# A hybrid encoder block on one core: conditioning sums spread over a sweep, decayed queries in another buffer group, block sums formed midway, and the last pair of tiles in its own order

## The chip, the cores and the metric

The kernel runs on one core of one Trainium2 chip. The metric is the device time of one execution in microseconds (us). Three runs of the kernel before took 2403.71 to 2405.92 us, with a median of 2404.65 us.

## What is computed

One encoder layer over 16 prompt tiles and 2 sample tiles of 128 rows each, with d = 1024, four retention heads of 128, and an MLP of width 4096:

```python
mod = silu(c) @ ada_w + ada_b                 # six vectors of 1024 per sequence
h = modulate(rmsnorm(x, norm_mix), sh1, sc1)
u, q, k, v, g = split(h @ w_in)
f = real(fft2(u over sequence and group)) @ w_fnet     # per group
r = retention(rotary(q), rotary(k), v, forward) + retention(..., backward, strict)
r = r * rsqrt(mean(r * r)) * silu(g)
x = x + gt1 * (concat(f, r) @ w_out)
h = modulate(rmsnorm(x, norm_mlp), sh2, sc2)
x = x + gt2 * (square(relu(h @ w_mlp_in)) @ w_mlp_out)
y = rmsnorm(x, norm_final)
```

## The kernel before, in words

Matrix products run as three passes of rounded halves (hi times hi, hi times lo, lo times hi), so each operand is split by a cast on ACT and a subtraction on DVE (line 81). Small products of 128x128 run in plain float32, which the trace counts as two matmuls each. A timeline of the framework sets the order of the instructions on each engine; each engine then takes its queue in order. Loads and stores are issued by SP, whose queue is in order too.

The stages that matter here, with their stretch of the trace:

- Sweep 1 (50 to 220 us) projects u. **Sweep 2** (220 to 450 us, the loop over `order`, tiles 17, 16, 15 down to 0) projects v and k with `w_v` and `w_k`, turns k by its rotary angles (`rotary`, lines 228 to 230: three DVE operations `rt`, `kv`, `kv`), stores `kv` to memory (line 711), runs jobs of the Fourier part, and adds up the backward state (`state_b`). In between stand 32 pieces of the conditioning product (`ada_piece`): each loads 512 KB of `ada_w` into a buffer `ada` and runs two DVE operations of 128x1024 on it (`adacc`, lines 354 and 356). After eight pieces `ada_end` multiplies the sums by ones on PE and copies the result on ACT (`adas`, line 373).
- **Sweep 3** (450 to 755 us, tiles 0 to 17) loads `kv`, projects q and g, and calls `retention` for the tile before and `ret_norm` for the one before that. A tile's queries `q` (and the backward state beside them), its decayed queries `qx` (lines 758 and 760) and its gate `sg` (`silu`, line 859) are tiles of 4 KB per partition in the pool group with the tag `"F"`, of which `w_g` and the decay table `xi` hold all but three. Tag `"S"` is the larger group, used by `h`, `hhi`, `hlo`, `kv`, `ada` and others.
- The output projection follows (755 to 975 us), then **MLP1** (980 to 1671 us): three groups `c` of three pairs of row tiles, and for each of them eight column groups `q`, each giving two blocks of hidden units (`hid`). Products use a seven-product block scheme, so that MLP2 needs seven combinations of the hidden blocks: four are stored and three (`S2` to `S4`) are sums. For the last quarter of the hidden units (`r = 3`) the sums are made in MLP1 (`hs`, `hid`) and all seven are stored to `hidd`; for the others MLP2 makes them from `hr` with four DVE operations for each pair.
- **MLP2** (1671 to 2403 us): four quarters `r` of the hidden units, and nine pairs of row tiles in each. `load_mo` prepares the weights of a quarter from `w_mlp_out` (buffers `t`, `o1`, `o2` in `raw` and `rawb`, results `woB`, `woT`). With `r = 3` each pair is finished: multiplied by the gate, added to `x1`, normalized and stored. For the last pair `finish_block` and `finish_rows` do this block by block.

Of the kernel before, what the change touches and what calls it, by code (L numbers as in the profile page):

```python
# [15 lines left out]
P = 128  # L16
# [15 lines left out]
def encoder(ctx: ExitStack, tc: tile.TileContext, a):  # L32
# [656 lines left out]
    for n, t in enumerate(order):  # L689
# [8 lines left out]
        if n >= 1 and jobs:  # L698
            for f in jobs.pop(0):
                f()  # L700
        if n >= 1:
            ada_piece(*ada_jobs.pop(0))
        for _ in range(0 if n < 11 else 1 if n == 11 else 2 if n < 16 else 3):
            ada_piece(*ada_jobs.pop(0), "F")
        kv = t4("kv", "S")
# [6 lines left out]
        if t not in (0, 16):  # L712
            vz = t2("vz")
            pool.tensor_tensor(out=heads(vz), in0=heads(kv[:, 512:1024]),
                               in1=zc[:, 4:8].unsqueeze(2).to_broadcast([P, H, P]), op=ALU.mult)
            pend = (t, kv, vz)
        if n == 12:
            w_q = load_w_in(512, "V")
# [29 lines left out]
    def retention(t, kv, s_b, q, sg, s_f):  # L748
# [6 lines left out]
        act.copy(qk[:, 0:512], tq)  # L755
        qx = t4("qx", "F")
        if not first:
# [77 lines left out]
    for n, t in enumerate(order2):  # L835
# [25 lines left out]
        if 5 <= n < 13:  # L861
            load_w_out(n - 5)
        if n == NT - 2:
            fetch_d(0)
# [113 lines left out]

    NB = [4] * (NG - 1) + [7]
    hidd = [[dram([NPC, GJ, P, NB[r] * P], "hidd") for r in range(NG)] for _ in range(NC)]  # L980

# [39 lines left out]
    for c in range(NC):  # L1021
        if c:
            left = left_ops()
            for pr in range(NPC):
# [5 lines left out]
                form_left(left, pr, *hab, lambda s: wt("s", s, [P, 512], 4))  # L1030
        for q in range(8):
            w = load_mi(q)
            hid = [wt("hid", "hid", [P, NPC, 4, P], 3) for _ in range(2)]
            at, cp_ = [{}, {}], [{}, {}]
            for i, (ln, rn, bn) in enumerate(STEPS):
                for f in range(2):
# [19 lines left out]
                    elif i == 6:  # L1056
# [4 lines left out]
                        dst = hidd[c][j // GJ][:, j % GJ].rearrange("a p n -> p a n")  # L1061
                        if j // GJ == NG - 1:
                            x = wt("hs", "hs", [P, NPC, 3, P], 2)
                            s2, s3, s4 = (x[:, :, m] for m in range(3))
                            sub(s3, hf[:, :, 0], hf[:, :, 3])
                            add(hf[:, :, 3], hf[:, :, 3], hf[:, :, 2])
                        sp.dma_start(out=dst[:, :, 0:4 * P], in_=hf.rearrange("p a b s -> p a (b s)"))
                        if j // GJ == NG - 1:
                            sub(s2, hf[:, :, 3], hf[:, :, 0])
                            sub(s4, hf[:, :, 1], s2)  # L1070
                            sp.dma_start(out=dst[:, :, 4 * P:7 * P], in_=x.rearrange("p a b s -> p a (b s)"))
# [65 lines left out]

    def finish_block(b, y, x1, ss):
        dve.tensor_tensor(out=y, in0=y, in1=gate[:, halves(b)], op=ALU.mult)
        dve.tensor_tensor(out=y, in0=y, in1=x1[:, halves(b)], op=ALU.add)  # L1140
        act.activation(x1[:, halves(b)], y, AF.Square, accum_out=ss[:, b % 2:b % 2 + 1])  # L1141

    def finish_rows(t, y, ss):
        dve.tensor_tensor(out=ss[:, 2:3], in0=ss[:, 0:1], in1=ss[:, 1:2], op=ALU.add)
        r = rstd_from(ss[:, 2:3], 1, 1.0 / D)
        for b in range(2):
            yb = y[:, 512 * b:512 * b + 512]
            dve.scalar_tensor_tensor(out=yb, in0=yb, scalar=r[:, 0:1], in1=nf[:, halves(b)],
                                     op0=ALU.mult, op1=ALU.mult)
            sp.dma_start(out=xrows("y", t)[:, halves(b)], in_=yb)  # L1150

    for r in range(NG):
        w = load_mo(r)
        if r == NG - 1:
            gate = load_gate(1, 0, lambda s: v1(s, "rawb"))
            nf = v1("nf", "rawb")
            sp.dma_start(out=nf, in_=a["norm_final"].rearrange("(o c) -> o c", o=1).to_broadcast([P, D]))
        for pr in range(NT // 2):
            if r == NG - 1 and pr == NP // 2:
                gate = load_gate(1, 1, lambda s: v1(s, "rawb"))  # L1160
            c, pc = divmod(pr, NPC)
            hv = v1("hr", f"hr{pr % 2}").rearrange("p (j b s) -> p j b s", j=GJ, b=7)
            sp.dma_start(out=hv[:, :, 0:NB[r], :].rearrange("p j b s -> p j (b s)"),
                         in_=hidd[c][r][pc].rearrange("j p n -> p j n"))
            src = {n: hv[:, :, i] for i, n in enumerate(("A11", "A12", "A22", "S1", "S2", "S3", "S4"))}
            if NB[r] == 4:
                sub(src["S3"], src["A11"], src["S1"])
# [8 lines left out]
            if r == NG - 1:  # L1176
                x1 = [v1("x1", "raw") for _ in range(2)]
                for i in range(2):
                    sp.dma_start(out=x1[i], in_=x1d[2 * pr + i])
            at = {}  # L1180
            ss = [tsm([P, 4], "ss") for _ in range(2)] if end else None
            for i, (ln, rn, bn) in enumerate(STEPS):
# [12 lines left out]
                else:  # L1195
                    dve.tensor_tensor(out=acc[:, b_], in0=o, in1=acc[:, b_], op=ALU.add)  # L1196
                if end:
                    if i not in (0, 2, 3):
                        finish_block(b_, acc[:, b_], x1[b_ // 2], ss[b_ // 2])
                    if i > 4:  # L1200
                        finish_rows(2 * pr + b_ // 2, rows[b_ // 2], ss[b_ // 2])
                elif r == NG - 1 and i > 4:
                    finish_tile(2 * pr + b_ // 2, rows[b_ // 2], x1[b_ // 2])
# [77 lines left out]
```

## Time and profile before

| what | us |
|---|---|
| median of three runs | 2404.65 |
| the profiled execution, its own time | 2405.53 |
| its span on the engines | 2403.5 |
| PE busy (97% of the span) | 2326.6 |
| DVE busy (64%) | 1539.2 |
| ACT busy (42%) | 1004.5 |
| POOL busy (5%) | 115.8 |

A row of the timeline gives the start, the busy time, the engine, the line, the operation with what it writes and reads, and how many instructions follow one another; in brackets stands how long the engine sat idle before and what ended that. "PE proj L84" is a matmul that writes the projection bank; "SPq" is a transfer issued by SP. Matmuls are pipelined: a row of n matmuls lasts n steps and the rest of the last one.

### The profile page before, as it was taken

To read this page: it belongs to the slowest core of one execution; us is meant where nothing else is said; L and a number is where in the kernel's file an instruction comes from. 1 tells how busy PE (TensorE), PEld (TensorE's weight loads), DVE (VectorE), ACT (ScalarE), POOL (GpSimd) and SP (SyncE) were. 2 spreads that over 40 slices of the span, in tenths; PEclk is the share of its full clock that TensorE was granted. 3 is DMA by queue.
4 is the path that set the end of the run, shared out by engine and by line. 5 is a ranking of instruction groups with operands and counts; after the bars stand their busy time and mean duration, and the time that the engine had idled before them with its cause. 6 is when DMAs were issued, how large, how long until landed. Compare 5 with 4: busy or idle time off the path is not lost.

```text
span 2403.5 us, 30791 instructions
## 1 busy us (share of the span) xinstructions
PE 2326.6 (97%) x11905; PEld 2033.9 (85%) x11905; DVE 1539.2 (64%) x2254; ACT 1004.5 (42%) x1686; POOL 115.8 (5%) x191
## 2 busy tenths in 40 slices
PE   7999999999999999999999999999899999999998
PEld 4788887788887888999999999998787788787786
DVE  3676768535444754655785577557756867857788
ACT  4842222223333533555665566556334323224332
POOL 0101100011111000000000000000000000000000
PEclk9999999999999999999999999999999999999999
DMA  8647568433333455543453346433534545546774
GB/s 286 215 144 252 188 217 289 171 99 121 119 103 127 140 171 188 167 131 123 154 184 123 127 156 194 136 120 130 191 105 159 200 158 197 188 158 227 276 255 165
DMA packets 183866, 411.69 MB, mean 171 GB/s; under 512 B 12101, under 2 KB 80485, under 8 KB 176809
## 3 DMA queue, kind: packets, MB, share of 16 engines
q1 hardware_dynamic: 182136, 405.68, 49.2%
q0 software_dynamic: 1584, 4.06, 0.6%
q8 instruction: 93, 1.52, 0.3%
q14 instruction: 53, 0.43, 0.1%
HBM read 274.15 MB, written 135.54 MB: 170 GB/s over the span
## 4 chain that ended last, share of the span: by engine, by line
PE 77%; issue 9%; DVE 6%; DMA 5%; ACT 2%; POOL 1%; SPq 0%; POOLq 0%; DVEq 0%; ACTq 0%
PE mX L963 30%; PE proj L84 18%; PE mZ L963 15%; PE mY L963 7%; PE o L84 2%; DMA ada<-ada_w 1%; PE dft L84 1%; PE tr L745 1%; DMA hr<-hidd 1%; DVE woT L81 1%; PE kvf L84 1%; DVE adacc L356 1%; DVE woB L81 1%; PE sc L84 1%; DVE acc L1196 1%
## 5 line engine op out<-in xcount | busy, mean ns | idle before, releaser
L963 PE MATMUL mX<-woT,ho 128*128 128x512 f32 x1296 | 311.5, 390 | 3.7 <-ACT x L1141 1.5
L80 ACT CAST ho<-hr 128x512 fp32r<-128x512 f32 x252 | 153.1, 621 | 343.3 <-PE mX L963 208.7
L963 PEld LDWEIGHTS mX<-woT,ho 128*128 128x128 f32 x1296 | 242.8, 188 | 56.3 <-issue 1.9
L963 PE MATMUL mX<-opS,wT 128*128 128x384 f32 x1152 | 208.0, 334 | 0.0
L84 PE MATMUL proj<-whi,hhi 128*128 128x512 f32 x720 | 190.1, 402 | 18.3 <-ACT hhi L80 9.4
L963 PEld LDWEIGHTS mX<-opS,wT 128*128 128x128 f32 x1152 | 200.4, 188 | 0.0
L81 DVE TENSOR_TENSOR ho<-hr,ho 128x512 fp32r<-128x512 f32 x252 | 170.4, 687 | 39.7 <-ACT ho L80 39.5
L84 PE MATMUL proj<-wlo,hhi 128*128 128x512 f32 x720 | 185.2, 396 | 0.0
L84 PE MATMUL proj<-whi,hlo 128*128 128x512 f32 x720 | 184.4, 393 | 0.0
L84 PEld LDWEIGHTS proj<-whi,hhi 128*128 128x128 f32 x720 | 132.4, 190 | 47.4 <-ACT hhi L80 10.7
L84 PEld LDWEIGHTS proj<-wlo,hhi 128*128 128x128 f32 x720 | 136.1, 191 | 30.7 <-issue 2.5
L84 PEld LDWEIGHTS proj<-whi,hlo 128*128 128x128 f32 x720 | 133.1, 188 | 30.7 <-issue 4.2
L81 DVE TENSOR_TENSOR wB<-mr,wB 128x1024 fp32r<-128x1024 f32 x72 | 88.0, 1222 | 81.1 <-ACT wB L80 81.0
L1196 DVE TENSOR_TENSOR acc<-mX,acc 128x512 f32<-128x512 f32 x117 | 80.0, 687 | 68.5 <-PE mX L963 55.5
L963 PE MATMUL mY<-woB,ho 128*128 128x512 f32 x432 | 112.2, 396 | 10.0 <-ACT woB L80 6.8
L963 PE MATMUL mX<-woB,ho 128*128 128x512 f32 x432 | 110.8, 396 | 5.6 <-ACT ho L80 5.5
L963 PE MATMUL mZ<-woT,ho 128*128 128x512 f32 x432 | 108.9, 392 | 6.3 <-ACT woT L80 5.5
L105 POOL TENSOR_SCALAR rv<-ss 128x1 f32<-128x1 f32 (+1 forms) x72 | 17.9, 248 | 1885.8 <-ACT x L139 1391.9
L80 ACT CAST wB<-mr 128x1024 fp32r<-128x1024 f32 x72 | 75.4, 1047 | 76.0 <-PE mY L963 41.0
L963 PEld LDWEIGHTS mY<-woB,ho 128*128 128x128 f32 x432 | 81.7, 190 | 30.1 <-ACT woB L80 8.3
L963 PE MATMUL mY<-opA,wB 128*128 128x384 f32 x576 | 104.6, 334 | 2.3 <-DVE x L153 2.3
L963 PE MATMUL mX<-opA,wB 128*128 128x384 f32 x576 | 105.5, 334 | 0.0
(251 smaller groups left out, 4368.9 us busy)
## 6 DMA issues: line engine op xcount, KB each, us to landing
mr<-w_mlp_in SPq DMA_DIRECT2D x96, 512.0 KB
hidd<-hid SPq DMA_DIRECT2D x48, 768.0 KB
hr<-hidd SPq DMA_DIRECT2D x27, 1024.0 KB
accd<-acc SPq DMA_DIRECT2D x27, 1024.0 KB
acc<-accd SPq DMA_DIRECT2D x27, 1024.0 KB
ada<-ada_w SPq DMA_DIRECT2D x48, 512.0 KB
h<-hd SPq DMA_DIRECT2D x36, 512.0 KB
x<-x_prompt SPq DMA_DIRECT2D x32, 512.0 KB
```

The source lines that it names most:

```text
L80: act.copy(hi, src)
L81: dve.tensor_tensor(out=lo, in0=src, in1=hi.bitcast(F32), op=ALU.subtract)
L84: pe.matmul(out, l, r, start=first, stop=last)
L105: pool.tensor_scalar(out=v[:, :n], in0=ss[:, :n], scalar1=scale, scalar2=EPS, op0=ALU.mult, op1=ALU.add)
L356: dve.scalar_tensor_tensor(out=acc_[s_], in0=w, scalar=c2[:, k, s_:s_ + 1], in1=acc_[s_], op0=ALU.mult, op1=ALU.add)
L745: pe.transpose(o[:, hs], src[:, hs], ident)
L963: pe.matmul(out, l, r, start=first and fresh, stop=last, skip_group_check=not fresh)
L1196: dve.tensor_tensor(out=acc[:, b_], in0=o, in1=acc[:, b_], op=ALU.add)
```

## The change

1. In sweep 2 the conditioning pieces move from ahead of the projections to behind the rotary and the store of k. One piece stands in each tile from the second on, and a second one in each tile from n = 5 on, in place of one, two or three extra ones from n = 11 on. Two of the 32 pieces now fall into sweep 3.
2. `qx` is allocated in the larger group `"S"` instead of `"F"`.
3. In MLP1 the eight column groups run in the order `QS`, which puts the last quarter's two groups (6 and 7) fourth and fifth. The sums are also made there for the first quarter of the first three pairs (`c = 0`, `r = 0`).
4. The last pair of MLP2 gets a function of its own, `last_pair`: the second gate is loaded ahead (`gate_s`, in `raw`), the products of bank X run as two halves of 256 columns, gate and `x1` are applied before the last product instead of after it, and one half of each row is scaled on ACT.

```diff
@@ sweep 2
-        if n >= 1:
-            ada_piece(*ada_jobs.pop(0))
-        for _ in range(0 if n < 11 else 1 if n == 11 else 2 if n < 16 else 3):
-            ada_piece(*ada_jobs.pop(0), "F")
         kv = t4("kv", "S")
         pv = proj(hl, w_v)
...
             pend = (t, kv, vz)
+        if n >= 1:
+            ada_piece(*ada_jobs.pop(0))
+        if n >= 5:
+            ada_piece(*ada_jobs.pop(0), "S" if n < 11 else "F")
@@ retention
-        qx = t4("qx", "F")
+        qx = t4("qx", "S")
@@ sweep 3
+        if n and ada_jobs:
+            ada_piece(*ada_jobs.pop(0))
@@ MLP1
-    NB = [4] * (NG - 1) + [7]
-    hidd = [[dram([NPC, GJ, P, NB[r] * P], "hidd") for r in range(NG)] for _ in range(NC)]
+    NB = [[7 if r == NG - 1 or c + r == 0 else 4 for r in range(NG)] for c in range(NC)]
+    hidd = [[dram([NPC, GJ, P, NB[c][r] * P], "hidd") for r in range(NG)] for c in range(NC)]
+    QS = (2, 0, 1, 6, 7, 3, 4, 5)
-        for q in range(8):
+        for q in QS:
-                        if j // GJ == NG - 1:
+                        if NB[c][j // GJ] == 7:
@@ MLP2
+    def last_pair(src, acc, x1, rows, w):
...
+        def gate_add(b):
+            y = acc[:, b]
+            dve.tensor_tensor(out=y, in0=y, in1=gate[:, halves(b)], op=ALU.mult)
+            add(y, y, x1[b // 2][:, halves(b)])
+        def square(b, k, c=full):
+            act.activation(junk[:, c], acc[:, b][:, c], AF.Square, scale=1.0 / 32,
+                           accum_out=col(k))
...
+        def rows_out(k, rest, early, late):
+            pool.tensor_tensor(out=col(k), in0=col(k), in1=col(rest), op=ALU.add)
+            pool.tensor_tensor(out=col(k), in0=col(k), in1=mhalf[:, 0:1], op=ALU.pow)
+            r = col(k)
+            y = x1[early // 2][:, halves(early)]
+            act.activation(y, y, AF.Copy, scale=r)
+            dve.scalar_tensor_tensor(out=acc[:, late], in0=acc[:, late], scalar=r, in1=nf[:, halves(late)],
                                      op0=ALU.mult, op1=ALU.mult)
+            store(act, early, y)
+            store(sp, late, acc[:, late])
...
+                at[bn] = [(bank("X"), ha), (bank("X"), hb)] if bn == "X" else [(bank(bn), full)]
...
+                if i < 6:
+                    dve.tensor_tensor(out=y, in0=oo, in1=y, op=ALU.add)
+                else:
+                    t = v1("tg", "raw")[:, 0:256]
+                    dve.tensor_tensor(out=t, in0=oo, in1=gate[:, halves(b_)][:, c], op=ALU.mult)
+                    add(y, y, t)
+                    square(b_, 4 + n, c)
...
-            gate = load_gate(1, 0, lambda s: v1(s, "rawb"))
+            gate, gate_s = (load_gate(1, i, lambda s: v1(s, ("rawb", "raw")[i])) for i in range(2))
...
-                gate = load_gate(1, 1, lambda s: v1(s, "rawb"))
+                gate = gate_s
```

Three places show how the order of the instructions moves.

The first is DVE at the end of sweep 2, around the last two tiles; `kv_3796` before and `kv_3763` now are the same rotated keys (of tile 0). Before:

```order
L239 SCALAR_TENSOR_TENSOR sbn_3664<-sbn_3554,kvb_3659 128x128 x4
L356 SCALAR_TENSOR_TENSOR adacc_3675<-ada_3771,c_101,adacc_3675 128x1024
L356 SCALAR_TENSOR_TENSOR adacc_3673<-ada_3775,c_101,adacc_3673 128x1024
L356 SCALAR_TENSOR_TENSOR adacc_3675<-ada_3775,c_101,adacc_3675 128x1024
L239 SCALAR_TENSOR_TENSOR sbn_3756<-sbn_3664,kvb_3751 128x128 x4
L228 TENSOR_TENSOR rt_3850<-proj_3823,rope_3848 128x512
L229 TENSOR_TENSOR kv_3796<-proj_3823,rope_3848 128x512
L229 TENSOR_TENSOR q_3901<-qr_3902,rope_3904 128x512
L230 TENSOR_TENSOR kv_3796<-kv_3796,rt_3850 128x512
```

Now:

```order
L356 SCALAR_TENSOR_TENSOR adacc_3657<-ada_3823,c_101,adacc_3657 128x1024
L356 SCALAR_TENSOR_TENSOR adacc_3659<-ada_3823,c_101,adacc_3659 128x1024
L228 TENSOR_TENSOR rt_3817<-proj_3790,rope_3815 128x512
L229 TENSOR_TENSOR kv_3763<-proj_3790,rope_3815 128x512
L356 SCALAR_TENSOR_TENSOR adacc_3657<-ada_3827,c_101,adacc_3657 128x1024
L239 SCALAR_TENSOR_TENSOR sbn_3674<-sbn_3586,kvb_3669 128x128 x4
L356 SCALAR_TENSOR_TENSOR adacc_3659<-ada_3827,c_101,adacc_3659 128x1024
L230 TENSOR_TENSOR kv_3763<-kv_3763,rt_3817 128x512
L81 TENSOR_TENSOR hlo_3840<-h_3835,hhi_3839 128x1024
L239 SCALAR_TENSOR_TENSOR sbn_3756<-sbn_3674,kvb_3751 128x128 x4
```

The rotated keys of tile 0 now stand ahead of the last backward state and of the first query's rotation, with two sums between their operations; no conditioning sum stands behind them in sweep 2.

The second is one tile of sweep 3, on DVE and then on PE; `qx_5232` and `o_5241` are the decayed queries and the output of the same tile, `sg_5037` is the gate of the tile before it, `q_5292` the query of the tile after it. DVE before:

```order
L229 TENSOR_TENSOR q_5147<-qr_5148,rope_5150 128x512
L230 TENSOR_TENSOR q_5147<-q_5147,rt_5152 128x512
L228 TENSOR_TENSOR rt_5297<-qr_5293,rope_5295 128x512
L808 SCALAR_TENSOR_TENSOR sg_5037<-sg_5037,rr_5206 128x128 x4
L758 TENSOR_TENSOR qx_5232<-tr_5226,xi_3858 128x512
L760 TENSOR_TENSOR qx_5232<-tr_5226,xi_3858 128x512
L239 SCALAR_TENSOR_TENSOR sfn_5261<-sfn_5116,kvf_5256 128x128 x4
L81 TENSOR_TENSOR hlo_5340<-h_5192,hhi_5339 128x1024
L766 TENSOR_TENSOR qkT_5219<-sc_5235,dec_3856 128x512
```

DVE now:

```order
L808 SCALAR_TENSOR_TENSOR sg_5037<-sg_5037,rr_5206 128x128 x4
L229 TENSOR_TENSOR q_5292<-qr_5293,rope_5295 128x512
L230 TENSOR_TENSOR q_5292<-q_5292,rt_5297 128x512
L228 TENSOR_TENSOR rt_5442<-qr_5438,rope_5440 128x512
L758 TENSOR_TENSOR qx_5232<-tr_5226,xi_3833 128x512
L760 TENSOR_TENSOR qx_5232<-tr_5226,xi_3833 128x512
L239 SCALAR_TENSOR_TENSOR sfn_5261<-sfn_5116,kvf_5256 128x128 x4
L766 TENSOR_TENSOR qkT_5219<-sc_5235,dec_3831 128x512
L81 TENSOR_TENSOR hlo_5340<-h_5192,hhi_5339 128x1024
```

The three rotary operations moved from ahead of the gate's four to between these and the two of `qx`, and they are now those of the tile after. PE in the same tile, where each row of a projection is two matmuls; before:

```order
L84 MATMUL proj_5557<-wlo_3310,hhi_5339 128x512 x2
L84 MATMUL proj_5557<-whi_3291,hlo_5340 128x512 x2
L84 MATMUL proj_5557<-whi_3309,hlo_5340 128x512 x2
L84 MATMUL o_5241<-kv_5045,qkT_5219 128x128
L84 MATMUL o_5241<-sfn_5116,qx_5232 128x128
L84 MATMUL o_5241<-q_5147,qx_5232 128x128
L84 MATMUL proj_5592<-whi_3521,hhi_5339 128x512 x2
```

Now:

```order
L84 MATMUL proj_5557<-wlo_3352,hhi_5339 128x512 x2
L84 MATMUL o_5241<-kv_5045,qkT_5219 128x128
L84 MATMUL o_5241<-sfn_5116,qx_5232 128x128
L84 MATMUL o_5241<-q_5147,qx_5232 128x128
L84 MATMUL proj_5557<-whi_3333,hlo_5340 128x512 x2
L84 MATMUL proj_5557<-whi_3351,hlo_5340 128x512 x2
L84 MATMUL proj_5592<-whi_3553,hhi_5339 128x512 x2
```

The eight matmuls of the q projection with `hlo` moved from ahead of the output's products to behind them, so they now stand between the output and the gate's projection (`proj_5592`).

The third is DVE at the border of MLP1 and MLP2, where the weights of the first quarter and the first pair's hidden blocks are prepared. Before:

```order
L1052 TENSOR_TENSOR hid_14125<-mX_14141,c_14240 128x3x128
L81 TENSOR_TENSOR woB_14420<-o_14465,woB_14420 128x512
L236 TENSOR_TENSOR hr_14533<-hr_14533 128x4x128
L81 TENSOR_TENSOR ho_14540<-hr_14533,ho_14540 128x512
L1054 TENSOR_TENSOR hid_14124<-mZ_14212,c_14196 128x3x128
L233 TENSOR_TENSOR hr_14533<-hr_14533 128x4x128
...
L236 TENSOR_TENSOR hs_14310<-hid_14124 128x3x128
```

Now:

```order
L1058 TENSOR_TENSOR hid_14160<-mZ_14248,c_14232 128x3x128
L1058 TENSOR_TENSOR hid_14161<-mZ_14263,c_14246 128x3x128
L81 TENSOR_TENSOR ho_14560<-hr_14557,ho_14560 128x512
L236 TENSOR_TENSOR t_14511<-o_14512 128x512
L81 TENSOR_TENSOR ho_14577<-hr_14557,ho_14577 128x512
L81 TENSOR_TENSOR ho_14594<-hr_14557,ho_14594 128x512
```

The four operations on `hr` of the first pair and the eight on `hs` and `hid` of the last column groups no longer stand here.

## Rows read from the trace of the kernel before

**Rows 1.** Windows view, 400 to 450 us: length, then busy time of each engine.

```profile
400.00:450.00 50.00, 48.38 (x233) 34.99 (x232) 44.79 (x62) 7.07 (x10) 3.73 (x2) 1.00 0.60 206
```

**Rows 2.** Timeline, 394 to 459 us, the end of sweep 2.

```profile
398.51 0.70 PE L84 MATMUL proj<-whi,hhi 128*128 128x512 f32 x2 [3.34 <-DVE kv L229]
...
446.74 0.59 ACT L373 COPY adas<-ada 128x512 f32<-128x512 f32 x1 [15.87 <-PE ada L84]
...
448.46 0.68 DVE L230 TENSOR_TENSOR kv<-kv,rt 128x512 f32<-128x512 f32 x1
...
449.61 2.11 PE L84 MATMUL proj<-whi,hhi 128*128 128x512 f32 x8 [1.62 <-ACT hhi L80]
...
456.04 0.66 PE L745 MATMUL tr<-ident,kv 128*128 128x128 f32 x4 [1.58 <-DMA kv<-kvd]
```

**Rows 3.** Tile view of `adacc` and of `vz`: durations in ns, least, median, most.

```profile
L356 DVE SCALAR_TENSOR_TENSOR adacc<-ada,c,adacc x56: 1269/1275/2065, 186.3 to 439.4; 128x1024 f32<-128x1024 f32 x56
...
L714 POOL TENSOR_TENSOR vz<-kv,zc x14: 1029/1132/1900, 226.3 to 421.3; 128x512 f32<-128x512 f32 x14
```

**Rows 4.** Waits of PE, 500 to 700 and 700 to 980 us: total, times, longest.

```profile
PE proj L84 <- ACT sg L859: 4.6, 10, 0.5
...
PE proj L84 <- ACT sg L859: 0.9, 2, 0.5
```

**Rows 5.** Timeline, 534 us and 612 to 616 us, two tiles of sweep 3.

```profile
534.08 0.39 PE L84 MATMUL o<-kv,qkT 128*128 128x128 f32 x2
534.93 2.12 PE L84 MATMUL proj<-whi,hhi 128*128 128x512 f32 x8 [0.46 <-ACT sg L859]
...
612.29 0.49 PE L745 MATMUL tr<-ident,sg 128*128 128x128 f32 x3
...
613.24 0.69 DVE L758 TENSOR_TENSOR qx<-tr,xi 128x512 f32<-128x512 f32 x1 [3.18 <-ACT qkT L755]
...
613.75 1.06 PE L84 MATMUL sc<-qkT 128*128 128x128 f32 x8
613.85 0.68 DVE L760 TENSOR_TENSOR qx<-tr,xi 128x512 f32<-128x512 f32 x1
...
614.64 0.39 PE L84 MATMUL o<-sfn,qx 128*128 128x128 f32 x2
...
615.84 1.51 POOL L782 TENSOR_TENSOR vz<-kv,zc 128x512 f32<-128x512 f32 x1 [6.96 <-DMA mixd<-rT]
```

**Rows 6.** Chain of waits, 1655 to 1670 us: start, length, what.

```profile
1659.43 6.70 DMA hr<-hidd
```

**Rows 7.** Timelines of DVE, PE and SP, 1655 to 1706 us.

```profile
1676.77 0.55 DVE L236 TENSOR_TENSOR hs<-hid 128x384 f32<-128x384 f32 x1
...
1681.56 1.22 PE L963 MATMUL mZ<-woT,ho 128*128 128x512 f32 x2 [5.03 <-ACT woT L80]
1688.79 2.07 PE L963 MATMUL mY<-woB,ho 128*128 128x512 f32 x4 [6.01 <-ACT woB L80]
...
1705.05 1.21 PE L963 MATMUL mX<-woB,ho 128*128 128x512 f32 x4 [0.53 <-ACT ho L80]
...
1683.11 0.33 SPq L1109 DMA_DIRECT2D o<-w_mlp_out  x1
```

**Rows 8.** Windows view, 1680 to 1694 us; the figure 0.51 is the granted clock.

```profile
1680.00:1694.00 14.00, 6.26 (x13) 3.70 (x14) 14.00 (x26) 5.99 (x12) 0.00 (x0) 0.51 0.85 300
```

**Rows 9.** Timeline, 2386 to 2404 us, the end of the last pair.

```profile
2387.13 2.88 PE L963 MATMUL mX<-woT,ho 128*128 128x512 f32 x12
...
2391.51 3.00 PE L963 MATMUL mX<-woT,ho 128*128 128x512 f32 x12 [1.49 <-ACT x L1141]
...
2394.86 0.68 DVE L1196 TENSOR_TENSOR acc<-mX,acc 128x512 f32<-128x512 f32 x1
...
2397.03 0.63 ACT L1141 ACTIVATE x<-acc 128x512 f32<-128x512 f32 x1 [3.41 <-DVE acc L1140]
...
2398.89 1.41 DVE L1148 SCALAR_TENSOR_TENSOR acc<-acc,rr,nf 128x512 f32<-128x512 f32 x2 [0.94 <-POOL rr L108]
```

More of the change, by code (lines that the diff above doesn't have):

```diff
@@ L1136, in halves, with col, left_op, gain @@
         return slice(b % 2 * 512, b % 2 * 512 + 512)
[L1138 to L1148, printed above, removed]
-                                     op0=ALU.mult, op1=ALU.mult)
-            sp.dma_start(out=xrows("y", t)[:, halves(b)], in_=yb)
+    def last_pair(src, acc, x1, rows, w):
+        full, ha, hb = slice(0, 512), slice(0, 256), slice(256, 512)
+        s_lo, s_hi = tsm([P, 4], "ss"), tsm([P, 4], "ss")
+        ho = {}
+        junk = v1("tj", "raw")
+        def col(k):
+            return (s_lo, s_hi)[k // 4][:, k % 4:k % 4 + 1]
+        def left_op(i):
+            t = v1("ho", f"ho{nho[0] // 3 % 2}", F32R)
+            nho[0] += 1
+            ho[i] = t[:, 0:512], t[:, 512:1024]
+            split(src[STEPS[i][0]], *(x.rearrange("p (j s) -> p j s", j=GJ) for x in ho[i]))
+        def gate_add(b):
[5 more added lines that the diff above has]
+                           accum_out=col(k))
+        def gain(b):
+            dve.tensor_tensor(out=x1[b // 2][:, halves(b)], in0=acc[:, b], in1=nf[:, halves(b)], op=ALU.mult)
+        def store(eng, b, y):
+            eng.dma_start(out=xrows("y", NT - 2 + b // 2)[:, halves(b)], in_=y)
+        def rows_out(k, rest, early, late):
[5 more added lines that the diff above has]
+            dve.scalar_tensor_tensor(out=acc[:, late], in0=acc[:, late], scalar=r, in1=nf[:, halves(late)],
+                                     op0=ALU.mult, op1=ALU.mult)
+            store(act, early, y)
+            store(sp, late, acc[:, late])
+        left_op(0)
+        gate_add(2)
+        at = {}
+        for i, (ln, rn, bn) in enumerate(STEPS):
+            if i < 6:
+                left_op(i + 1)
+            if i in (0, 1, 3):
+                at[bn] = [(bank("X"), ha), (bank("X"), hb)] if bn == "X" else [(bank(bn), full)]
+            hh, hl = ho[i]
+            b_ = ADDR[i]
+            for n, (o, c) in enumerate(at[bn]):
+                oo = o[:, 0:c.stop - c.start]
+                three(lambda p_, j, first, last: add_mm(
+                    i, oo, (hh, hh, hl)[p_][:, j * P:(j + 1) * P], w[j][rn][p_ % 2][:, c], first, last), range(GJ))
+                y = acc[:, b_][:, c]
+                if i < 6:
+                    dve.tensor_tensor(out=y, in0=oo, in1=y, op=ALU.add)
[4 more added lines that the diff above has]
+                    square(b_, 4 + n, c)
+            if i == 1:
+                gate_add(0)
+                square(0, 0)
+                gain(0)
+                dve.tensor_scalar(out=col(6), in0=col(0), scalar1=EPS, scalar2=None, op0=ALU.add)
+            elif i == 4:
+                gate_add(3)
+                square(3, 3)
+                gain(3)
+            elif i == 5:
+                gate_add(1)
+                square(1, 1)
+                rows_out(1, 6, 0, 1)
+            elif i == 6:
+                dve.tensor_scalar(out=col(7), in0=col(3), scalar1=col(4), scalar2=EPS,
+                                  op0=ALU.add, op1=ALU.add)
+                rows_out(5, 7, 3, 2)
@@ L1159, in encoder @@
             if r == NG - 1 and pr == NP // 2:
-                gate = load_gate(1, 1, lambda s: v1(s, "rawb"))
+                gate = gate_s
             c, pc = divmod(pr, NPC)
             hv = v1("hr", f"hr{pr % 2}").rearrange("p (j b s) -> p j b s", j=GJ, b=7)
-            sp.dma_start(out=hv[:, :, 0:NB[r], :].rearrange("p j b s -> p j (b s)"),
+            sp.dma_start(out=hv[:, :, 0:NB[c][r], :].rearrange("p j b s -> p j (b s)"),
                          in_=hidd[c][r][pc].rearrange("j p n -> p j n"))
             src = {n: hv[:, :, i] for i, n in enumerate(("A11", "A12", "A22", "S1", "S2", "S3", "S4"))}
-            if NB[r] == 4:
+            if NB[c][r] == 4:
                 sub(src["S3"], src["A11"], src["S1"])
@@ L1179, in encoder @@
                     sp.dma_start(out=x1[i], in_=x1d[2 * pr + i])
+            if end:
+                last_pair(src, acc, x1, rows, w)
+                break
             at = {}
-            ss = [tsm([P, 4], "ss") for _ in range(2)] if end else None
             for i, (ln, rn, bn) in enumerate(STEPS):
@@ L1196, in encoder @@
                     dve.tensor_tensor(out=acc[:, b_], in0=o, in1=acc[:, b_], op=ALU.add)
[L1197 to L1202, printed above, removed]
+                if r == NG - 1 and i > 4:
                     finish_tile(2 * pr + b_ // 2, rows[b_ // 2], x1[b_ // 2])
```

2 lines of the change are left out of this document (1 added, 1 removed).

## Prediction, made blind

> **What bounds the kernel now.** I read the page first: PE is busy 97% of the span, so a gain can only come from one of PE's remaining idle places or from the tail behind its last product. The next views were the waits of PE by stretch and the timelines around the waits that they name, since the four parts of the change touch four such places.
>
> The end of sweep 2: DVE is busy 44.8 of the 50 us from 400 to 450 [rows 1], and its queue holds the conditioning sums back to back, 1.275 us each [rows 3]. Rotary operations stand behind them, so PE waits 3.34 us for a bank that the rotary of k has not yet read, ACT idles 15.87 us in front of the copy `adas` because the sums behind it are late (the next cast of `h` and PE behind it lose 1.62 us), and the last keys are rotated at 448.46 only, which makes their store and reload late and costs 1.58 us at a transposition [rows 2]. That is 6.5 us.
>
> Sweep 3: in 12 tiles the gate's projection waits for ACT, 5.5 us together [rows 4]: `sg` may write its buffer only when the previous tile's output has read the `q` or `qx` in it, and the output's products stand directly ahead of that projection. In one tile the last two of them start at 534.08; two steps of 0.11 us later would be 534.30, and the projection's first matmul starts at 534.93 [rows 5], so that the tile loses 0.63 us of issue time and 12 tiles 7.6 us.
>
> The border of MLP1 and MLP2: PE loses 5.03, 6.01 and 0.53 us to weights and hidden blocks that are not ready [rows 7], and the granted clock is 0.51 from 1680 to 1694 us, the lower of the two levels [rows 8]. DVE is busy all of these 14 us [rows 8].
>
> The tail: PE waits 1.49 us ahead of the last product, and 8.6 us lie from 2394.86, when DVE takes that product, to the end of the span [rows 9].
>
> **Part 1, the sums.** The work is the same: 64 operations of 1.275 us and 32 loads. By the order, DVE between two successive `hlo` of the last tiles had, in sums of own durations, 14.3, 13.4, 11.2, 15.4, 7.1 and 24.4 us, and now has 12.7, 10.3, 11.6, 14.1, 9.0 and 19.1, with 12.3 and 1.9 after them. Working these forward in order from the twelfth tile, I find every rotary ahead of the bank that PE wants by 3 us or more, the last keys rotated about 10 us before their transposition (they need 7.6: from 448.46 to 456.04 [rows 2]), and `adas` no longer in front of the first casts of sweep 3. So the 6.5 us go. What is late next is the middle of the sweep, where two pieces now stand in tiles that had one (up to 18.8 us of DVE in a tile whose two projections hold PE about 11 us, with Fourier jobs beside them); I keep 0.5 us for it. **−6.0 us**, bounds 0 (the waits return elsewhere) and −8 (small losses nearby go as well). The queue of SP carries the same 32 loads, in tiles where it has fewer others.
>
> **Part 2, `qx` in the other group.** With `qx` gone, `q` and `sg` alternate over three buffers: `sg` still takes that of the previous tile's `q`, but the next `q` takes that of the gate before, which is free after its transposition. By the order the output's products now run 8 matmuls ahead of the gate's projection; at 0.226 us each (2.88 us for 12, less 0.39 for the last alone, by 11 [rows 9]) that is 1.8 us, more than 0.63. The old wait goes: −7.6.
>
> In its place stands a queue. DVE now has the three rotary operations of the following tile between the gate's four and the two of `qx`, and the first of these three waits until PE has transposed all of the gate, since it writes that gate's buffer. In the tile of rows 5 the three last transpositions of the gate start at 612.29 and end at 612.78. In the new order the last of them is the tenth of the twelve steps, 0.22 earlier, 612.56. DVE starts at 612.61. Its operations of this size take 0.69 us and follow each other in 0.61 where independent (613.24 to 613.85 [rows 5]) and in about 0.72 where the second needs the first: 613.33, 613.94, and `qx` at 614.55 instead of 613.24, done at 615.24, the second at 615.84. PE's order has the first product of the output directly behind the scores, ready at 614.64 [rows 5]. It waits 0.63 us with its restart, and the next product 0.38 more for the second half of `qx`. That is 1.0 us in a tile, and the order has this sequence in 12 tiles: +12.1. Queued behind these are `sfn`, `qkT` and `hlo`, which PE needs 16 matmuls (3.6 us) later, so they add nothing. **+4.5 us** net. Bounds: −7.6 if DVE comes in time after all, +7 if each tile loses 0.2 more.
>
> The two pieces that go to sweep 3 are 2.5 us of DVE each in the second and third tile, where DVE is far from full; and in one late tile the output's products lose the matmuls that stood between them. I take **+1 us**, from 0 to +2.
>
> **Part 3, the block sums.** In MLP1 16 operations of about 0.5 us are added to the first group, beside a PE that waits for none of them; their cover is DVE's idle time there. At the border eight such operations (0.47 us of queue each) and the four on `hr` leave. Against that stands the first pair's load, 1.79 MB instead of 1.02 MB: it took 6.70 us [rows 6], and 0.77 MB more at the 300 GB/s of rows 8 is 2.6 us; with the traffic ahead of it I take 3.2. ACT and DVE stand blocked on it. Between `load_mo`'s first operation and the one that frees the buffer of the last `o2`, DVE has 37 operations instead of 44, which is 4.2 us less at 0.60. So that load, issued at 1683.11 [rows 7] and the cause of the 6.01 us, goes out about 1 us earlier. The 0.53 us at 1705 go, and another 1 us where DVE no longer mixes `hs` with the weights. **−2.5 us**, bounds −5 (all operations that left count) and +2 (the load is as late as its bytes, and nothing else moves). The low clock remains, since PE still idles over 5 us ahead of it.
>
> **Part 4, the last pair.** Loading the gate ahead removes DVE's wait. Of PE's 1.49 us [rows 9] about 1.0 goes, since DVE's finishing of the pair before still stands in front. Four products of 12 matmuls become 24 half-width ones, 0.01 to 0.02 us more for two halves: +0.6. Behind the last matmul, three DVE operations (the distance from 2394.86 to ACT's square at 2397.03 is 2.17 us [rows 9]) become two of half width, about 0.85, and one of the two row scalings (0.66) goes to ACT, early: −1.9. **−2.3 us**, bounds −1 and −4. `gate_s` holds one of the buffers for the `x1` loads of all nine pairs, which I cost at nothing: they are covered by a pair's 19 us of PE work.
>
> **The sum** is −6.0 + 4.5 + 1 − 2.5 − 2.3 = −5.3 us. The profiled execution took 2405.53 us, 0.9 above the median of the runs, and would take 2400.2; from the median of 2404.65 it gives 2399.3 us.
>
> **Rivals.**
>
> *Sweep 3 runs clean.* If DVE's `qx` is not late, because the gate's transpositions come earlier or the rotary does not wait, the 12.1 us of part 2 are not paid: −17.4, 2387 us. For it: before, DVE sat idle 3.18 us ahead of `qx` [rows 5]. Against it: the order has the rotary behind that wait in every one of these tiles.
>
> *Sweep 2 keeps its losses elsewhere.* The pieces now stand right behind `vz`, and their loads need buffers of a group that `qx` shares. Then part 1 gives nothing: +0.7, 2405 us, no change. This is also the case that the change does not do what it says, if the loads come late and the sums bunch again.
>
> *Slower: `vz` meets the rotary in sweep 3.* Beside `vz` the sums have taken 2.065 us instead of 1.275, and `vz` 1.900 instead of 1.03 [rows 3]. In sweep 3 `vz` ran at 615.84, after a store of `rT` [rows 5]. If it starts between 612.6 and 614.5, one of the three rotary operations ahead of `qx` waits for 0.79 to 1.03 us of it, and the output with it: 9.5 to 12.4 us in 12 tiles, 2408.8 to 2411.7 us. That store would have to land 1.3 us earlier or more; the new order moves the copy of `rT` ahead by one operation of ACT, about 0.5 us, so I give it little. The Trainium skill, page "SBUF — State Buffer", section "SBUF: two separate sides", says that VectorE with two SBUF inputs and a GpSimd operation that reads SBUF share a port pair as an exclusive lock, held for a whole instruction. By that rule the loser would pay all that is left of the other; the longest sum of rows 3 agrees, the median shows that most do not meet.
>
> **How the numbers follow.** Forecast as summed 0.60, sweep 3 clean 0.15, sweep 2 no better 0.17, `vz` 0.08. The first one's own range is 2394 to 2404. About 0.2%, 4.8 us, can be told from no change: 2399.8 and 2409.5 are the borders. The forecast lies just under the first, so I give 0.35 of its 0.60 to faster; with sweep 3 clean that makes 0.50. Slower is most of the `vz` case and a little of the others, 0.09; the rest, 0.41, is no change. The range reaches down to the clean sweep 3 at 2387 and up to 2406, just above the case without sweep 2's gain.
>
> **What would show it.** In the trace after: PE's 3.3 and the two 1.6 us waits of sweep 2 gone; in sweep 3 no wait of the projection on `sg`, but a wait of `o` on `qx` of 0.5 to 1 us in some 12 tiles; the 6.01 us wait at the border shorter by about 1; from the last product to the end of the span some 7 us. I am wrong on part 2 if `o` never waits for `qx`, on part 1 if projections in sweep 2 still wait for `kv`, and on part 3 if the first `hr` of 1.79 MB lands so late that PE's waits at the border grow.

## The result, and the profile after

Four runs of the changed kernel took 2388.39 to 2390.80 us, median 2389.52; the kernel before, run beside it, took 2403.71 to 2405.92, median 2404.24. The ratio is 0.9933 with a 95% interval of 0.9921 to 0.9945: 14.7 us less by the medians, nearly three times the forecast's 5.3. The time lies inside the stated range (2387 to 2406) and beyond the likeliest case's own (2394 to 2404). It lies near the 2387 of the rival in which sweep 3 runs clean, but sweep 3 does not run clean, as the rows below show.

The tile views of three names give the first start of their matmuls, and so cut the span in the same places of both kernels. `kvf` starts with sweep 3's first retention, `mX<-opA` with MLP1, `mX<-woB` with MLP2. The changed kernel:

```profile
L84 PE MATMUL kvf<-vz,kv x128: 270/275/348, 443.3 to 749.7; 128*128 128x128 f32 x128
L965 PE MATMUL mX<-opA,wB x576: 333/334/420, 958.5 to 1637.1; 128*128 128x384 f32 x192
L965 PE MATMUL mX<-woB,ho x444: 278/389/628, 1662.2 to 2360.7; 128*128 128x512 f32 x140, 128*128 128x256 f32 x8
```

And the kernel before:

```profile
L84 PE MATMUL kvf<-vz,kv x128: 270/275/377, 457.3 to 753.8; 128*128 128x128 f32 x128
L963 PE MATMUL mX<-opA,wB x576: 333/334/423, 967.5 to 1646.1; 128*128 128x384 f32 x192
L963 PE MATMUL mX<-woB,ho x432: 387/389/794, 1671.2 to 2375.1; 128*128 128x512 f32 x144
```

| stretch | before, us | changed, us | difference |
|---|---|---|---|
| start to the first `kvf` (sweeps 1 and 2) | 457.3 | 443.3 | −14.0 |
| to MLP1's first product (sweep 3, output projection) | 510.2 | 515.2 | +5.0 |
| MLP1 | 703.7 | 703.7 | 0 |
| MLP2 to the end of the span | 732.3 | 725.3 | −7.0 |
| span | 2403.5 | 2387.5 | −16.0 |

**Sweep 2.** PE's waits from 200 to 500 us in the changed kernel (total, times, longest):

```profile
PE proj L84 <- ACT kv L703: 1.8, 1, 1.8
PE proj L84 <- ACT hhi L80: 0.2, 1, 0.2
```

The same stretch of the kernel before had six waits, 8.5 us. Three of them were in the forecast [rows 2]; two more stood at its start, on the Fourier part:

```profile
PE dft L84 <- ACT zh L80: 1.3, 1, 1.3
PE dft L84 <- DVE zl L81: 0.5, 1, 0.5
```

So 6.5 us of waits went, and not all of them where the forecast looked. The windows view at that early place shows what followed those two: the granted clock (the figure behind POOL) was 0.76 on average from 233 to 240 us,

```profile
233.00:240.00 7.00, 5.18 (x26) 4.49 (x26) 3.60 (x4) 3.06 (x4) 1.04 (x1) 0.76 0.89 312
```

and is 1.00 in the changed kernel, where PE is busy through all of the 7 us:

```profile
233.00:240.00 7.00, 7.00 (x49) 6.42 (x48) 4.51 (x9) 3.55 (x5) 0.00 (x0) 1.00 0.79 253
```

That is 0.24 of 7 us, 1.7 us more in this execution. It is no fixed price of the two waits: the run with part 3's order alone, which has the sums of the kernel before and the same two waits (1.3 and 0.5 us), shows a clock of 1.00 there and no low stretch in sweep 2. Such a stretch stands in the sweep 2 of four of the five profiles with the old sums, at 233 us or between 390 and 410 us, and in two of the eight with the new numbers. A third part is no wait at all. PE's timeline before, at one conditioning product, with the projection that it interrupts:

```profile
389.01 1.05 PE L84 MATMUL ada<-adacc,ones 128*32 128x512 f32 x4
389.99 0.96 PE L84 MATMUL proj<-wlo,hhi 128*128 128x512 f32 x3
390.88 1.05 PE L84 MATMUL ada<-adacc,ones 128*32 128x512 f32 x4
```

and in the changed kernel:

```profile
411.28 1.06 PE L84 MATMUL ada<-adacc,ones 128*32 128x512 f32 x8
412.28 0.96 PE L84 MATMUL proj<-whi,hhi 128*128 128x512 f32 x3
```

A run of four takes 0.98 us of PE's queue (389.01 to 389.99), and a run of eight 1.00 us (411.28 to 412.28). The products of the two sequences write different rows of one bank, and side by side they cost once. Before, three of the four conditioning products were split, because the sums of the second sequence came later: 3 us by these rows. Two further runs, with 2 us, have only moved into sweep 3. Together −6.5, −1.7, −3 and −2 make −13.2 of the −14.0 between these two executions.

**Sweep 3.** PE's waits from 500 to 700 us, where it had waited for `sg` [rows 4]:

```profile
PE o L84 <- DVE qx L758: 3.0, 9, 0.3
```

One tile of it on DVE and PE, which answers to [rows 5]:

```profile
636.91 0.38 PE L745 MATMUL tr<-ident,sg 128*128 128x128 f32 x2
...
637.33 0.69 DVE L229 TENSOR_TENSOR q<-qr,rope 128x512 f32<-128x512 f32 x1 [3.61 <-PE tr L745]
...
638.05 0.69 DVE L230 TENSOR_TENSOR q<-q,rt 128x512 f32<-128x512 f32 x1
...
638.51 1.16 PE L84 MATMUL sc<-qkT 128*128 128x128 f32 x8
638.66 0.68 DVE L228 TENSOR_TENSOR rt<-qr,rope 128x512 f32<-128x512 f32 x1
...
639.27 0.68 DVE L758 TENSOR_TENSOR qx<-tr,xi 128x512 f32<-128x512 f32 x1
...
639.87 0.68 DVE L760 TENSOR_TENSOR qx<-tr,xi 128x512 f32<-128x512 f32 x1
...
640.00 0.49 PE L84 MATMUL o<-sfn,qx 128*128 128x128 f32 x2 [0.34 <-DVE qx L758]
...
640.60 0.49 PE L84 MATMUL o<-q,qx 128*128 128x128 f32 x2
...
640.85 2.10 PE L84 MATMUL proj<-whi,hhi 128*128 128x512 f32 x8
...
656.58 1.16 PE L84 MATMUL sc<-qkT 128*128 128x128 f32 x8
```

The same two places in the kernel before, behind the scores at 613.75 [rows 5]:

```profile
615.01 2.08 PE L84 MATMUL proj<-whi,hhi 128*128 128x512 f32 x8
...
631.45 1.06 PE L84 MATMUL sc<-qkT 128*128 128x128 f32 x8
```

DVE's rotary waits for the gate's transposition, and the two operations of `qx` stand behind all three: starts of 637.33, 638.05, 638.66, 639.27, 639.87, the steps of the forecast to 0.01 us. The output's products start at 640.00 and 640.60. From the scores to the projection behind these products PE takes 2.34 us (638.51 to 640.85), where it took 1.26 (613.75 to 615.01). From one tile's scores to the next tile's it is 18.07 us in place of 17.70, since the wait for `sg` is gone from the same tiles.

**The border and the end.** PE's waits from 1640 to 1720 us, before 12.7 us in sum:

```profile
PE mX L965 <- ACT acc L1269: 4.5, 1, 4.5
PE mZ L965 <- ACT woT L80: 4.2, 1, 4.2
PE mZ L965 <- ACT ho L80: 1.2, 1, 1.2
```

They are 9.9 us now. The granted clock is 0.74 on average over the 20 us from 1664, where in the kernel before it was 0.69 over the 22 us from 1672; that is another 1.6 us, and it differs between executions, as the last section shows. The last product waits 0.32 us in place of 1.49, and from its start to the end of the span it is 2387.5 − 2376.39 = 11.1 us in place of 2403.5 − 2391.51 = 12.0 [rows 9]:

```profile
2376.39 3.10 PE L965 MATMUL mX<-woT,ho 128*128 128x256 f32 x24 [0.32 <-DVE acc L1201]
```

### The profile page after: what moved, and what is told of

Same layout as the page of the kernel before. It is cut to its first block, busy times and chain, and to the rows that moved or that the text cites. A ratio compares the mean times of both kernels' runs of the same rounds, so it can differ in the third digit from the quotient of the medians.

```text
span 2387.5 us, 30934 instructions
## 1 busy us (share of the span) xinstructions
PE 2323.4 (97%) x11953; PEld 2037.7 (85%) x11953; DVE 1536.2 (64%) x2264; ACT 1010.0 (42%) x1690; POOL 112.5 (5%) x191
## 5 line engine op out<-in xcount | busy, mean ns | idle before, releaser
L965 PE MATMUL mX<-woT,ho 128*128 128x512 f32 (+1 forms) x1332 | 312.4, 384 | 7.0 <-ACT acc L1269 4.5
L965 PE MATMUL mX<-woB,ho 128*128 128x512 f32 (+1 forms) x444 | 110.8, 388 | 5.1 <-ACT ho L80 4.5
L965 PE MATMUL mZ<-opS,wT 128*128 128x384 f32 x576 | 104.3, 334 | 0.0
```

The lines of the kernel that those rows point to most:

```text
L965: pe.matmul(out, l, r, start=first and fresh, stop=last, skip_group_check=not fresh)
```

## The experiments

Each was timed beside the kernel before. The theories were formed after the result: nearly all of the gain is sweep 2's and the border's, and part 2 is a loss. Most runs take one part, or half of one, alone or leave it out; the last ones try a version without either wait of sweep 3.

**Part 1 alone.**

```diff
-        if n >= 1:
-            ada_piece(*ada_jobs.pop(0))
-        for _ in range(0 if n < 11 else 1 if n == 11 else 2 if n < 16 else 3):
-            ada_piece(*ada_jobs.pop(0), "F")
         kv = t4("kv", "S")
...
             pend = (t, kv, vz)
+        if n >= 1:
+            ada_piece(*ada_jobs.pop(0))
+        if n >= 5:
+            ada_piece(*ada_jobs.pop(0), "S" if n < 11 else "F")
...
+        if n and ada_jobs:
+            ada_piece(*ada_jobs.pop(0))
```

> Part 1 alone, in the kernel before. Theory: nearly all of the gain sits in sweep 2 and needs nothing of the other parts: 11 to 13 us less than before (about 2392), with PE's waits on kv, hhi and the reloaded kv gone and fewer, longer runs of the conditioning matmuls between projections. Rival: the sums can only be spread because qx has left the F group, and alone they give the 6 us of the blind forecast or less (2398 or more). In sweep 3 both expect the old wait of the projection on sg, 0.5 us in 12 tiles.

Measured: 2395.91 us beside 2406.50, ratio 0.9955 (0.9943 to 0.9968): 10.6 us less. The tile views:

```profile
L84 PE MATMUL kvf<-vz,kv x128: 269/276/348, 444.6 to 743.2; 128*128 128x128 f32 x128
L965 PE MATMUL mX<-opA,wB x576: 333/335/687, 955.6 to 1638.1; 128*128 128x384 f32 x192
L965 PE MATMUL mX<-woB,ho x432: 388/390/795, 1663.2 to 2366.0; 128*128 128x512 f32 x144
```

Sweep 2's end is 12.7 us earlier, and MLP1's first product 11.9. So the part stands on its own, as the theory had it, a little under the theory's 11 to 13 us. MLP1 then takes 707.6 us in place of 703.7: at its entry PE waits 4.1 us for the transposed `x` (2.3 before), and the granted clock falls behind that:

```profile
962.00:970.00 8.00, 7.90 (x31) 7.87 (x32) 7.34 (x10) 2.16 (x5) 0.13 (x1) 0.63 0.59 212
```

Of 11.9 us won, 3.9 are given back there in this execution.

**Which half of part 1.** First the old numbers at the new place:

```diff
-        if n >= 1:
-            ada_piece(*ada_jobs.pop(0))
-        for _ in range(0 if n < 11 else 1 if n == 11 else 2 if n < 16 else 3):
-            ada_piece(*ada_jobs.pop(0), "F")
         kv = t4("kv", "S")
...
             pend = (t, kv, vz)
+        if n >= 1:
+            ada_piece(*ada_jobs.pop(0))
+        for _ in range(0 if n < 11 else 1 if n == 11 else 2 if n < 16 else 3):
+            ada_piece(*ada_jobs.pop(0), "F")
```

> The kernel before with the conditioning pieces moved behind the rotary and the store of k, but in the old numbers (one, then two to four in the last tiles). Theory, that the even numbers carry the gain of part 1: the last tiles keep most of their waits, and only the split runs of the conditioning matmuls (0.95 us each, three of them) and part of the waits go: 3 to 6 us less than before. Rival, that the place behind the rotary carries it: 9 us less or more, as in the run with the whole of part 1.

Measured: 2406.50 beside 2405.62, ratio 1.0000 (0.9991 to 1.0009): nothing, less than both expected. Its waits in sweep 2 only change place, 8.4 us in place of 8.5:

```profile
PE adat L381 <- ACT adas L373: 2.9, 1, 2.9
PE proj L84 <- DVE kv L229: 2.4, 1, 2.4
PE proj L84 <- ACT qr L853: 1.8, 1, 1.8
PE proj L84 <- ACT kv L703: 0.7, 1, 0.7
PE proj L84 <- ACT hhi L80: 0.6, 1, 0.6
```

All four conditioning products run unsplit here, in runs of eight at 304.71, 400.49, 429.85 and 451.70 us. By the rows above that should give 3 us, and MLP1's first product comes only 0.6 us earlier (966.9 us). In this execution a clock of 0.83 on average from 380 to 400 us took some 3 us, where the kernel before lost 1.7 in its sweep 2. So the price of the split runs rests on the rows, and no run shows it in the time.

Then the new numbers at the old place:

```diff
         if n >= 1:
             ada_piece(*ada_jobs.pop(0))
-        for _ in range(0 if n < 11 else 1 if n == 11 else 2 if n < 16 else 3):
-            ada_piece(*ada_jobs.pop(0), "F")
+        if n >= 5:
+            ada_piece(*ada_jobs.pop(0), "S" if n < 11 else "F")
         kv = t4("kv", "S")
...
+        if n and ada_jobs:
+            ada_piece(*ada_jobs.pop(0))
```

> The kernel before with the new even numbers of conditioning pieces, but ahead of the projections as before. Theory, that the even numbers carry the gain of part 1: 8 to 11 us less than before, most of what the whole of part 1 gives. Rival, that the place behind the rotary carries it: 4 us or less, with the projection still waiting for the rotary of k in the late tiles.

Measured: 2398.19 beside 2405.62, ratio 0.9968 (0.9955 to 0.9980): 7.4 us less, a little under the theory's 8 to 11 and above the rival's 4. The waits of sweep 2 fall to 3.0 us:

```profile
PE proj L84 <- DVE kv L229: 1.9, 1, 1.9
PE proj L84 <- ACT kv L707: 0.7, 2, 0.4
PE ada L84 <- DVE adacc L356: 0.4, 1, 0.4
```

So the even numbers carry most of the gain. With them come the two pieces that move to sweep 3 and the group `"S"` for the second pieces up to n = 10, which no run separates. Whether the place adds to it is not shown: the whole part gave 10.6 us and the numbers alone 7.4, each beside other runs of the kernel before, and the intervals overlap.

**Part 2 alone.**

```diff
-        qx = t4("qx", "F")
+        qx = t4("qx", "S")
```

> Part 2 alone, in the kernel before. Theory: it trades the wait of the projection on sg (0.74 us of issue time in each of 12 tiles) for a wait of the output on qx (about 1.07): 3 us slower than before, 2407 to 2408, with no wait on sg left and o waiting for qx twice in a tile. Rival: with qx in the larger group the sweep runs better, 3 us or more faster than before.

Measured: 2410.83 beside 2406.50, ratio 1.0016 (1.0007 to 1.0025): 4 us slower. The trace has no wait on `sg` from 500 to 700 us and this one in its place:

```profile
PE o L84 <- DVE qx L758: 3.0, 9, 0.3
```

The mechanism and the sign of the forecast's part 2 are shown in the kernel before, with a net price close to its +4.5.

**Part 2 undone.** In the changed kernel:

```diff
-        qx = t4("qx", "S")
+        qx = t4("qx", "F")
```

> The changed kernel with qx put back into the F group, the other three parts kept. Theory: 2 to 4 us faster than the changed kernel, about 2386.5, the old waits on sg back and no wait on qx. Rival: the spread sums need the larger group for qx, and the time goes back up to 2393 or more.

Measured: 2391.72 beside 2406.50, ratio 0.9939 (0.9927 to 0.9952), which cannot be told from the changed kernel: the theory's 2 to 4 us did not come, nor the rival's loss. In the trace MLP1 starts 5.4 us earlier than in the changed kernel and lasts 2.5 us longer, again with a wait of 4.1 us at its entry (2.1 in the changed kernel):

```profile
L965 PE MATMUL mX<-opA,wB x576: 331/335/690, 953.1 to 1634.2; 128*128 128x384 f32 x192
L965 PE MATMUL mX<-woB,ho x444: 278/390/629, 1659.3 to 2360.0; 128*128 128x512 f32 x140, 128*128 128x256 f32 x8
```

MLP2 takes the other 2.7 us: 728.0 us to the end of the span. The changed kernel itself has taken 725.3 and, profiled again, 728.2, so that this part is spread. The 4.1 us at MLP1's entry are not spread: they stand in all four builds that change the sums and keep `q`, `qx` and `sg` in group `"F"` (this one, part 1 alone and both halves of it), and in every other profile that wait is 2.0 to 2.4 us. So beside part 1, part 2 gives back at the entry of MLP1 a good part of what it costs in sweep 3. Why that entry waits longer in these builds was not tried.

**Part 3, whole and in half.** Whole, in the kernel before:

```diff
-    NB = [4] * (NG - 1) + [7]
+    NB = [[7 if r == NG - 1 or c + r == 0 else 4 for r in range(NG)] for c in range(NC)]
...
+    QS = (2, 0, 1, 6, 7, 3, 4, 5)
...
-        for q in range(8):
+        for q in QS:
```

> Part 3 alone, in the kernel before: the order of the column groups and the sums for the first three pairs. Theory: the border of MLP1 and MLP2 loses 3.5 to 4.5 us less, nothing else moves: 2.5 to 5 us less than before. Rival: the longer first load (1.79 MB) takes back what the operations gain, and the time is within 1 us of before.

Measured: 2399.50 beside 2405.62, ratio 0.9978 (0.9968 to 0.9988): 5 to 6 us less. PE's waits at the border, 10.2 us in place of 12.7:

```profile
PE mX L963 <- ACT acc L1196: 4.9, 1, 4.9
PE mZ L963 <- ACT woT L80: 4.2, 1, 4.2
PE mZ L963 <- ACT ho L80: 1.1, 1, 1.1
```

The rest in this execution is the clock, 0.77 on average from 1672 to 1694 us where it was 0.69, and waits between 1720 and 1950, 1.1 us less. Only the order:

```diff
-        for q in range(8):
+        for q in QS:
```

> Of part 3 only the order of the column groups, in the kernel before; the first three pairs' sums stay in MLP2. Theory, that what counts is to have the last quarter's sums (eight operations of 0.47 us) out of the border: 3 to 5 us less than before, most of what part 3 gave. Rival, that the four operations on the first pair's blocks count: 0 to 2 us less.

Measured: 2400.77 beside 2406.00, ratio 0.9977 (0.9968 to 0.9986): the same gain. Its clock from 1672 to 1694 us is 0.69, as before, and PE's waits alone are less: 9.4 us at the border in place of 12.7, and 20.0 in place of 26.0 from MLP2's first product to the end. So the gain does not need the faster clock. The order does it; what the first pairs' sums add, four operations fewer against 0.77 MB more in the first load, cannot be told from nothing.

**Part 4 alone.** `last_pair` as in the changed kernel, and the early gate, in the kernel before:

```diff
+            if end:
+                last_pair(src, acc, x1, rows, w)
+                break
...
-                gate = load_gate(1, 1, lambda s: v1(s, "rawb"))
+                gate = gate_s
```

> Part 4 alone, in the kernel before. Theory: PE's wait ahead of the last product shrinks by about 1 us and the tail behind it by 1.2, less 0.5 for the half-width products: 1 to 2.5 us less than before. Rival: the buffer that the second gate holds through the last quarter delays the loads of the pairs, and the time is the same or longer.

Measured: 2404.53 beside 2405.62, ratio 0.9997 (0.9988 to 1.0005): unclear. Its own places show the gain, a wait of 0.32 us ahead of the last product and 11.3 us from its start to the end of the span in place of 12.0, so 1.8 us:

```profile
2392.87 3.10 PE L963 MATMUL mX<-woT,ho 128*128 128x256 f32 x24 [0.32 <-DVE acc L1197]
```

but MLP2 as a whole took 732.5 us in that execution (732.3 before), and the clock from 2040 to 2060 us was 0.83 (0.91 before).

**A version without either wait of sweep 3.** The experiments left one place where the changed kernel loses and should not: of `q`, `qx` and `sg`, the one to leave group `"F"` can be `sg`.

```diff
-        qx = t4("qx", "S")
+        qx = t4("qx", "F")
-        sg = t4("sg", "F")
+        sg = t4("sg", "S")
```

> The changed kernel with qx back in the F group and the gate sg in the larger group S instead. In the order, neither the projection has to wait for a buffer that the output still reads, nor do the rotary operations stand ahead of qx. Theory: both waits of sweep 3 vanish, about 1.0 us in each of 12 tiles, so 2377 to 2381, faster than the changed kernel by 8 to 12 us. Rival: a gate lives longer than qx, so S runs short and h, kv or the raw weights load late: 2388 or more, with PE waiting for transfers or hhi in sweep 3.

Measured: 2385.45 beside 2406.50, ratio 0.9914 (0.9900 to 0.9927): faster than the changed kernel, by about half of what the theory had. It was repeated beside the changed kernel on one chip.

> The changed kernel once more, beside the versions with sg in S, so that they are compared on one chip. Expected: 15 to 16 us less than before, as in its first runs; the two versions with sg in S some 4 to 6 us below it if the first look at that version was right, level with it if that was this chip's spread.

Measured: 2390.72 beside 2406.00, ratio 0.9936 (0.9923 to 0.9950).

> The changed kernel with qx in the F group and sg in the S group, once more on the same chip as the changed kernel. Theory: both waits of the middle of sweep 3 are gone, 4 to 6 us less than the changed kernel. Rival: within 2 us of it.

Measured: 2384.64, ratio 0.9912 (0.9898 to 0.9926): 6.1 us below the changed kernel. DVE's queue in one tile shows why, `qx` ahead of the rotary:

```profile
632.42 0.69 DVE L758 TENSOR_TENSOR qx<-tr,xi 128x512 f32<-128x512 f32 x1 [2.66 <-ACT qkT L755]
...
633.63 0.68 DVE L229 TENSOR_TENSOR q<-qr,rope 128x512 f32<-128x512 f32 x1
```

From 500 to 700 us PE now loses 0.5 us. MLP1's first product comes at 949.0 us, 9.5 earlier than in the first profile of the changed kernel; MLP1 and MLP2 are 1.2 and 1.5 us longer than there. One loss is left at the end of the sweep:

```profile
719.80 0.33 PE L745 MATMUL tr<-ident,sg 128*128 128x128 f32 x1 [2.96 <-DVE sg L808]
```

The last version puts the last four gates back:

```diff
-        sg = t4("sg", "S")
+        sg = t4("sg", "S" if n < 14 else "F")
```

> As the version with sg in S, but the last four tiles' gates in F again, since in that version PE loses 3.1 us at 717 us, at the first transposition of a late gate. Theory, that the late gate comes from the S group running short at the end of the sweep: another 2 to 3 us less. Rival, that the order of DVE's queue makes the gate late whichever group it lies in: no change within 1 us, or the old waits of 0.6 us back in the last tiles.

Measured: 2383.30 beside 2406.00, ratio 0.9905 (0.9892 to 0.9919). The late gate costs 1.9 us in place of 3.0, and one old wait of 0.5 us on `sg` is back, so neither account holds whole. The 1.3 us to the version ahead cannot be told from the spread. Its interval lies clear below that of the changed kernel: this is the best version found, 7.4 us under it and 22.7 under the kernel before.

## Why the prediction was right and wrong

**Direction and range** held; the likeliest time was 10 us too high. Step by step:

- **Part 1, −6.0.** This step failed in size. Alone it gave 10.6 us, and in the trace 11.9 us by MLP1's first product. The forecast counted three waits, 6.5 us, and kept 0.5 for new ones. Gone are 8.5 us of waits against 2.0 new ones, so 6.5 net, close to its 6.0. What it left at nothing was not on the waits view as a loss of these sums: the split runs of conditioning products (3 us by the rows), which the order shows, the 2 us of runs that only move to sweep 3, and the low clock behind the two early waits (1.7 us in that execution, and none in another build with the same waits). How the gain in the time divides among these was not isolated. What was "late next" came true in kind: one wait of 1.8 us for the copy of v at 387 us.
- **Part 2, +4.5.** The mechanism is right, with the steps of DVE's queue to 0.01 us. PE loses 1.08 us in a tile between the scores and the projection (2.34 less 1.26) for a forecast of 1.01, and a tile is 0.37 us longer (18.07 less 17.70) for a forecast of 1.01 − 0.63 = 0.38. Only the count is less: the waits view has nine such waits in sweep 3, not 12. Alone it measured +4 us; beside the other three parts it cannot be told from nothing.
- **+1 for the end of sweep 3.** In sweep 3 and the output projection together it was +5.0: 2.0 for two runs of conditioning products that moved there, some 2.1 up to the scores of the fourteenth tile (at 692.39, before at 702.26, so 9.9 us ahead), and 0.9 from there to MLP1's first product (9.0 ahead), close to this term.
- **Part 3, −2.5.** Mis-sized: 5 to 6 us alone. The forecast priced the load of the last `o2` (1 us earlier) and two small items. The waits at the border fell by 2.5 to 3.3 us, about as priced, and those between 1720 and 1950 us by about 1 more. The low clock remained, as the forecast had said, and was shorter in some executions; since the order alone gained as much at the old clock of 0.69, it is no necessary part of the gain. The half of the part on which it spent its working, the longer first load against four operations, makes no measurable difference.
- **Part 4, −2.3.** In its own places 1.8 us, in the time unclear (0.9997). The wait ahead of the last product gave 1.17 us for the forecast's 1.0; the tail was mis-sized, 0.7 to 0.9 us for 1.9. From DVE's last reading of the bank (2379.97) to the end of the span it is 7.5 us, before 8.6, forecast some 7.
- **The rivals.** The time is nearest to the clean sweep 3, and only the trace tells that this rival is false: `o` waits for `qx` in the sweep. Sweep 2 did not keep its losses. And `vz` did not meet the rotary: the view of source line 229 from 500 to 700 us (least, median, most in ns) has no longer one, and lines 228 and 230 have none above 685 and 694.

```profile
L229 DVE TENSOR_TENSOR q<-qr,rope x11: 691/692/693, 512.3 to 691.2; 128x512 f32<-128x512 f32 x11
```

The parts alone add up to −10.6 + 4.3 − 6.1 − 1.1 = −13.5 us by their medians; the whole was −14.7 and −15.3 in its two sets of runs. That sum agrees within the spread, which does not show that the parts add one by one: without part 2 the other three give −17.8 by their own runs, and the run with part 2 undone gave −14.8, a difference that the intervals leave open. Against the forecast, the surplus is 4.6 us of part 1 and 3.6 of part 3.

## What to carry to other kernels

When a change spreads side work over a loop, count from the order and the trace the waits that go and the pieces into which the side work's own matmuls are cut. The stretches of low clock behind waits can go with them, but here they came and went between builds with the same waits. When a buffer is moved to another group, look at who inherits its slot and at what stands behind that one in its engine's queue; here the wait moved from PE's projection to DVE's rotary and came back to PE as a late `qx`, and moving another tile of the same size avoided both. What a part costs alone need not be what it costs beside the others: part 2 was +4 us alone, and beside the other three it could not be told from nothing. A time that matches a rival's number is no evidence for the rival until its place in the trace has been looked at.

## What the runs showed of the hardware

A run of matmuls that each write 32 rows of a bank took as long for two products as for four: 0.98 us for four instructions and 1.00 for eight, as the rows above show. The Trainium skill, page "TensorEngine Tiling (Array Packing)", section "Available Configurations", lists four tiles in the configuration 128x32. The trace agrees, as far as two pairs side by side cost what one does.

The granted clock was not the same in two executions of one kernel. From 1664 to 1684 us the changed kernel had 0.74 in its first profile and 0.67 in its second,

```profile
1664.00:1684.00 20.00, 10.12 (x34) 6.81 (x33) 18.58 (x31) 13.94 (x24) 0.00 (x0) 0.74 0.71 264
```

```profile
1664.00:1684.00 20.00, 9.52 (x25) 6.19 (x26) 18.29 (x31) 14.97 (x26) 0.00 (x0) 0.67 0.67 243
```

and MLP2 took 725.3 and 728.2 us in them. Differences of 3 us between single executions of these kernels are no evidence, and the small parts were judged by the intervals over several runs.
